# A hybrid attention block with a SwiGLU layer on one core: row sums fetched ahead through another queue, and eight score products at full width

## The chip, the cores and the metric

The kernel runs on one core of a Trainium2 chip. The metric is the device time of one execution in microseconds. The engines are named as in the profile: PE is TensorE, with PEld for its weight loads, DVE is VectorE, ACT is ScalarE, POOL is GpSimd and SP is SyncE, which here only issues DMAs.

## The reference

One decoder layer on 256 tokens of width 2048, float32. The input is normalised and projected once. One part of the projection feeds four heads of gated linear attention, another eight heads of sparse attention. Both outputs go through one output projection, and a SwiGLU layer with 5632 hidden columns follows. Cut to what matters here:

```python
n = rms_norm(x, attn_norm_g)
proj = n @ w_in
...
# gated linear attention, per chunk: b is the running sum of the log decay
decay = exp(where(causal, b[t] - b[s], -inf))
scores = einsum('bhtd,bhsd,bhtsd->bhts', qi, ki, decay)
...
h = x + concatenate([gla_out, nsa_out], axis=-1) @ w_out
m = rms_norm(h, ffn_norm_g)
return h + (silu(m @ w_gate) * (m @ w_up)) @ w_down
```

## The kernel before

**Numbers in two parts.** Every large product is made from operands split into a high part and the rest. ScalarE writes the high part (`hi`, line 136 or 623), VectorE the rest (`lo`, line 137 or 624), and TensorE makes three products of each pair of tiles: high by high, high by low, low by high. So each weight tile passes through ScalarE, then VectorE, then TensorE.

**Order of the work.** The kernel is written as Python generators. `drive` steps a main stream of products and lets side work (`urgent`, `later`) advance between them; a third list, `background`, gives one step every so many units. A planner then lays the instructions out on the engines; where a tile pool has no free buffer, the instruction that fills the next one waits until the readers of the oldest are done.

**Linear attention.** The decay between two tokens is handled by levels. `LEVELS` is 0, 1, 2, 4, ..., 64; level 0 is the diagonal, and at level l the tokens are cut into blocks of 2 l, of which the second half looks at the first. `gla_scores` does one head and one tile of 128 tokens: two banks of four products each, one for each level, every one a 128x128 product of which a mask keeps the entries that belong to the level. At the top level, l = 64, one 64x64 corner is all that is kept, and there the product itself is cut to that corner (line 565): 64 columns of weights and 64 columns of the other operand. The corner is then copied into the scores without a mask (line 574). There are 8 such products, each two records in the trace.

**The FFN.** The hidden columns are done in eleven blocks of 512 (`fb` 0 to 10). In a block, `gate_up` goes over eight pairs of 128 rows of the weights. It uses a scheme of seven products where eight would be plain: three with the weights themselves, four with sums of weight tiles. So for each pair there are three loaded parts to split and four sums. The sums `s1` and `s2` (two tiles each) are made on VectorE (lines 1104 to 1106), except that for blocks 5 to 10 those of pairs 2, 5 and 7 (`SUMS`) have been made early, in the `background` list during the attention, and put into DRAM by `sum_rows` (line 1018, from GpSimd's queue). In those blocks the kernel fetches the finished sums (line 1099) from SP's queue, behind the loads of the same pair (`load4`, line 1041):

```python
r = load4([(w_gate[0], a, 2, fb * FB), (w_up[0], a, 1 if ready else 2, fb * FB)])
if ready:
    sums = s1, s2 = g4([2, 512]), (fw["sum"] if fw else g4)([2, 512])
    for to, part in zip(sums, ready):
        nc.sync.dma_start(to, part)
```

Buffers: `fw["sum"]` (in the trace `fsum`, for `s2`) has 2, loaded weights (`fraw`) 3, split parts (`ftwo`) 4. `g4` (in the trace `g`, for `s1`) has 24, most of which hold lasting data in the FFN. After `gate_up` of a block comes `down` of the block before: four loads of `w_down`, 96 products at line 282. The products of `gate_up` are at line 1073.

Of the kernel before, what the change touches and what calls it, by code (L numbers as in the profile page):

```python
# [15 lines left out]
P = 128  # L16
# [20 lines left out]
def kernel(  # L37
# [4 lines left out]
    nc = tc.nc  # L42
    act, mm = nc.scalar.activation, nc.tensor.matmul
# [14 lines left out]
    def slot(pool, tag, bufs, align=None):  # L58
        def f(shape, dt=F32):
            n_tiles[0] += 1  # L60
            return pool.tile([P] + list(shape), dt, tag=tag, bufs=bufs, name=f"{tag}_{n_tiles[0]}", align_bytes=align)
        return f
# [3 lines left out]
    g4, g2, g1, small = slot(gp, "g4", 24, LINE), slot(s2p, "g2", 13), slot(s1p, "g1", 7), slot(s1p, "sm", 12)  # L66

    def bank():
        n_tiles[0] += 1
        return pp.tile([P, 512], F32, tag="bank", name=f"bank_{n_tiles[0]}")  # L70
# [21 lines left out]
    def drain(queue):  # L92
        while queue:
            for _ in queue.pop(0):
                pass
# [20 lines left out]
    def weight(tag, nk, w, bufs, dt=F32R):  # L116
        n_tiles[0] += 1
        if tag == "raw":
            t = wp.tile([P, 4 * 536], dt, tag=tag, bufs=bufs, name=f"{tag}_{n_tiles[0]}")
            return t[:, :nk * w].rearrange("p (k w) -> p k w", w=w)  # L120
        line = LINE // 4
        t = wp.tile([P, 2, 9 * line], dt, tag=tag, bufs=bufs, name=f"{tag}_{n_tiles[0]}", align_bytes=LINE)
        return t[:, :nk, :w]
# [432 lines left out]
    def gla_scores(h, b, res):  # L556
        tb = slice(b * P, (b + 1) * P)
        sc, e = g1([P]), dec[h // 2]
        for half in range(2):
            p = bank()  # L560
            for j in range(4):
                l = LEVELS[4 * half + j]
                u, w = (e[l][:, h % 2, tb],) * 2 if l else (kT[:, h, tb], qT[:, h, tb])
                if 2 * l == P:
                    mm(p[:l, j * P + l:(j + 1) * P], u[:, :l], w[:, l:], start=True, stop=True)
                else:
                    mm(p[:, j * P:(j + 1) * P], u, w, start=True, stop=True)  # L567
                yield
            for j in range(4):
                l, pl = LEVELS[4 * half + j], p[:, j * P:(j + 1) * P]  # L570
                if l == 0:
                    TT(sc, pl, lmask[:, 0, :], ALU.mult)
                elif 2 * l == P:
                    nc.vector.tensor_copy(sc[:l, l:], pl[:l, l:])
                else:
                    nc.vector.copy_predicated(sc, lmask[:, 4 * half + j, :].bitcast(mybir.dt.uint32), pl)
        res["s"] = sc
# [423 lines left out]
    row_sums = {}  # L1001
# [22 lines left out]
    fw = {}  # L1024

    def ffn_pools():
        nonlocal g2, small
        for pool in (wp, s2p, s1p, cp):
            pool.release()
        fr = ctx.enter_context(tc.tile_pool(name="fr", bufs=1, reuse_waits="tile"))  # L1030
        fs = ctx.enter_context(tc.tile_pool(name="fs", bufs=1, reuse_waits="tile"))
        fp = ctx.enter_context(tc.tile_pool(name="fp", bufs=1, reuse_waits="tile"))
        fw["sum"] = slot(fs, "fsum", 2)
        fw["raw"], fw["two"] = slot(fr, "fraw", 3, LINE), slot(fp, "ftwo", 4, LINE)
        g2, small = slot(fs, "f2", 6), slot(fs, "fm", 4)

    def load4(parts):

        r, at = fw["raw"]([4, 512]) if fw else weight("raw", 4, 512, 3, F32), 0
        for mat, k0, nk, c0 in parts:  # L1040
            nc.sync.dma_start(r[:, at:at + nk], mat[k0 * P:(k0 + nk) * P, c0:c0 + 512].rearrange("(k p) w -> p k w", p=P))
            at += nk
        return r
# [14 lines left out]
    def parts_of2(s1, s2):  # L1058
# [2 lines left out]
            in_parts(hi[:, 2 * i:2 * i + 2], lo[:, 2 * i:2 * i + 2], v)  # L1061
        return [(hi[:, k], lo[:, k]) for k in range(4)]


    banks = {}

    def gate_up(fb):
        def product(q, a, w, k):

            if q not in banks:  # L1070
                banks[q] = bank()
            for x, m in ((a[0], w[k][0]), (a[0], w[k][1]), (a[1], w[k][0])):
                mm(banks[q], x, m, start=todo[q] == total[q], stop=todo[q] == 1)  # L1073
                todo[q] -= 1

        def tokens(k, t):
            assert k in turned
            return tuple(x[k // 4][:, k % 4, t * P:(t + 1) * P] for x in (hT_h, hT_l))

        order, sevens = (ORDER0, ORDER1, ORDER)[0 if fb == 0 else 1 if fb < ALL7 else 2], FIRST7.get(fb, PAIRS7)  # L1080
        last7 = max(sevens, key=order.index)
        todo = dict.fromkeys((1, 5, 6, 7), 3 * len(sevens))
        todo.update(dict.fromkeys((2, 3, 4), 3 * len(sevens) + 6 * (8 - len(sevens))))
        todo[8] = 6 * (8 - len(sevens))
        total = dict(todo)
        if fb > 1:
            urgent.append(turn_act(fb - 1, (8, 8)))
        for at, pair in enumerate(order):
            if fb > 1 and pair not in sevens:
                drain(urgent)  # L1090
            if fb == 0 and at == len(OLD):
                ffn_pools()
            a, b = 2 * pair, 2 * pair + 1
            ready = row_sums.get((fb, pair))
            r = load4([(w_gate[0], a, 2, fb * FB), (w_up[0], a, 1 if ready else 2, fb * FB)])
            if ready:
                sums = s1, s2 = g4([2, 512]), (fw["sum"] if fw else g4)([2, 512])
                for to, part in zip(sums, ready):
                    nc.sync.dma_start(to, part)
            if pair in sevens:  # L1100
                w = parts_of(r[:, 0:3])
                if not ready:
                    s1, s2 = g4([2, 512]), fw["sum"]([2, 512])
                    TT(s1, r[:, 1:3], r[:, 3:4].to_broadcast([P, 2, 512]), ALU.add)  # L1104
                    TT(s2[:, 0], s1[:, 1], r[:, 1], ALU.add)  # L1105
                    TT(s2[:, 1], s2[:, 0], r[:, 0], ALU.add)  # L1106
                f = [tuple(forms[pair][:, i, j] for i in range(2)) for j in range(4)]
                raw = {1: (tokens(b, 0), 1), 2: (tokens(a, 0), 0), 3: (f[3], 2)}
                of_sums = {5: (f[0], 0), 7: (f[2], 1), 6: (f[1], 2), 4: (tokens(a, 1), 3)}

                for q in (6, 1, 5, 7, 2, 3, 4) if at == 7 else (1, 2, 3, 5, 7, 6, 4):
                    if q in of_sums and len(of_sums) == 4:
                        ws = parts_of2(s1, s2)
                        if ready:
                            ws = [ws[k] for k in (1, 0, 3, 2)]
                    if q in raw:
                        x, k = raw[q]
                        product(q, x, w, k)
                    else:
                        x, k = of_sums.pop(q)  # L1120
                        product(q, x, ws, k)
                    yield 2
            else:
                w = parts_of(r)
                for q, t, m in ((2, 0, 0), (3, 0, 1), (4, 1, 0), (8, 1, 1)):
                    for j in range(2):
                        product(q, tokens(a + j, t), w, 2 * m + j)
                        yield 2
            if pair == last7:
                q1, u, q5u, q7u, q57u = (g2([512]) for _ in range(5))  # L1130
                act(q1, banks[1], AF.Copy)
                TT(u, banks[6], q1, ALU.add)
                TT(q5u, banks[5], u, ALU.subtract)
                TT(q7u, banks[7], u, ALU.add)  # L1134
                TT(q57u, banks[5], q7u, ALU.subtract)
                if fb == 1:
                    urgent.append(turn_act(0, (1, 5)))
                if fb:
                    seed(0, DOWN[min(fb - 1, 1)])
        if fb == 0:  # L1140
            drain(urgent)
            rms(rf, ssh)
            TT(rf, rf, hback, ALU.mult)
        gs = hidden[fb] = []
        for t, (g, gq, u_, uq) in enumerate(((q1, 2, q5u, 3), (q7u, 4, q57u, 8))):
            TT(g, banks[gq], g, ALU.add)
            act(g, g, AF.Silu, scale=rf[:, t:t + 1])
            if total[uq]:
                TT(u_, banks[uq], u_, ALU.add)
            STT(g, u_, rf[:, t:t + 1], g, ALU.mult, ALU.mult)  # L1150
            gs.append(g)
# [184 lines left out]
```

## Time and profile before

| | before |
|---|---|
| median of 3 runs | 1117.23 us (1116.94 to 1117.36) |
| profiled execution | 1116.86 us, span 1115.2 us |
| TensorE busy | 1106.1 us, 99% of the span |
| VectorE busy | 993.3 us, 89% |
| ScalarE busy | 741.0 us, 66% |
| GpSimd busy | 50.1 us, 4% |
| granted TensorE clock | 1.00 |
| moved by DMA | 265.39 MB, mean 238 GB/s |

In rows of the timeline the first column is the start in us from the span's start, the second the length, then engine, line, operation, tiles and count; what stands in brackets is how long the engine sat idle before it and who ended that. In rows that group a line's instructions, three durations are the least, the median and the greatest in ns. `PEld` rows are weight loads, which overlap the products. `SPq` is SP's queue.

### The profile page before, as it was taken

How to read it: one execution, taken by the hardware profiler on the slowest of the kernel's cores; microseconds unless marked ns; L12 is line 12 of the kernel's file. 1: busy time of each engine (PE TensorE's matmuls, PEld its weight loads, DVE VectorE, ACT ScalarE, POOL GpSimd, SP SyncE). 2: the span in 40 equal slices, each digit the busy share in tenths (PEclk: the TensorE clock that was granted, in tenths of full speed). 3: DMA queues.
4: the chain of work that ended last, by engine and by line, in shares of the span. 5: the costliest groups of instructions: out<-in, count | busy, mean ns of one | idle time of the engine just before them, and what ended most of it. 6: DMA issues, size and time to landing. Idle time of an engine off the chain costs nothing.

```text
span 1115.2 us, 14712 instructions
## 1 busy us (share of the span) xinstructions
PE 1106.1 (99%) x5354; PEld 908.0 (81%) x5354; DVE 993.3 (89%) x1294; ACT 741.0 (66%) x1001; POOL 50.1 (4%) x97
## 2 busy tenths in 40 slices
PE   9999999999999999999999999999999999999998
PEld 8888887898778887887888888888888788888886
DVE  6678779987588889999899999899999999999997
ACT  7655557544576486657586676768686776768694
POOL 3110000111001000000000000000000000000000
PEclk9999999999999999999999999999999999999999
DMA  7999984475884786646465746767666767766763
GB/s 272 346 343 368 354 284 167 136 247 179 274 303 165 240 303 223 239 175 236 154 214 178 244 159 212 249 227 249 233 245 237 262 207 274 256 245 229 250 226 113
DMA packets 127795, 265.39 MB, mean 238 GB/s; under 512 B 6838, under 2 KB 8922, under 8 KB 127723
## 3 DMA queue, kind: packets, MB, share of 16 engines
q1 hardware_dynamic: 121642, 244.50, 63.4%
q0 software_dynamic: 5184, 18.88, 4.2%
q10 hardware_dynamic: 896, 1.07, 0.3%
q8 instruction: 42, 0.69, 0.2%
q14 instruction: 31, 0.25, 0.1%
HBM read 243.45 MB, written 20.97 MB: 237 GB/s over the span
## 4 chain that ended last, share of the span: by engine, by line
PE 94%; DVE 2%; ACT 2%; DMA 1%; issue 1%; POOL 0%; ACTq 0%; POOLq 0%; DVEq 0%
PE bank L282 46%; PE bank L1073 39%; PE bank L209 3%; PE bank L1214 2%; PE bank L883 1%; PE bank L567 1%; DVE lo L137 1%; PE bank L821 1%; DMA raw<-in_w_in_dram 1%; DMA raw<-in_w_out_dram 0%; ACT hi L136 0%; PE bank L737 0%; ACT ftwo L623 0%; POOL sm L212 0%; PE bank L824 0%
## 5 line engine op out<-in xcount | busy, mean ns | idle before, releaser
L1073 PE MATMUL bank<-ftwo,g 128*128 128x512 f32 x1848 | 431.7, 393 | 0.2 <-ACT ftwo L623 0.2
L1073 PEld LDWEIGHTS bank<-ftwo,g 128*128 128x128 f32 x1848 | 342.0, 188 | 77.1 <-DVE ftwo L624 3.1
L282 PE MATMUL bank<-hi,g 128*128 128x512 f32 (+2 forms) x1088 | 323.5, 376 | 0.0
L624 DVE TENSOR_TENSOR ftwo<-fraw,ftwo 128x1536 fp32r<-128x1536 f32 (+1 forms) x130 | 256.9, 1983 | 7.1 <-ACT ftwo L623 6.1
L623 ACT ACTIVATE ftwo<-fraw 128x1536 fp32r<-128x1536 f32 (+1 forms) x130 | 216.4, 1669 | 26.5 <-DMA fraw<-in_w_up_dram 10.0
L282 PE MATMUL bank<-ftwo,g 128*128 128x512 f32 x960 | 221.2, 390 | 0.4 <-ACT g L623 0.4
L282 PEld LDWEIGHTS bank<-hi,g 128*128 128x128 f32 x1088 | 192.4, 188 | 30.7 <-issue 1.0
L282 PEld LDWEIGHTS bank<-ftwo,g 128*128 128x128 f32 x960 | 179.5, 188 | 39.4 <-ACT bank L1185 1.3
L136 ACT ACTIVATE hi<-raw 128x1024 fp32r<-128x1024 f32 (+3 forms) x124 | 130.1, 1056 | 106.4 <-PE bank L282 62.7
L282 PE MATMUL bank<-lo,g 128*128 128x512 f32 (+3 forms) x544 | 195.3, 377 | 1.2 <-DVE lo L137 1.0
L137 DVE TENSOR_TENSOR lo<-raw,hi 128x1024 fp32r<-128x1024 f32 (+3 forms) x124 | 150.1, 1218 | 37.1 <-ACT hi L136 32.3
L623 ACT ACTIVATE ftwo<-g 128x1024 fp32r<-128x1024 f32 x74 | 78.3, 1058 | 75.9 <-DVE g L1104 60.4
L282 PEld LDWEIGHTS bank<-lo,g 128*128 128x128 f32 x544 | 98.5, 188 | 16.9 <-DVE lo L137 2.0
L624 DVE TENSOR_TENSOR ftwo<-g,ftwo 128x1024 fp32r<-128x1024 f32 x74 | 90.3, 1220 | 15.7 <-ACT ftwo L623 15.7
L624 DVE TENSOR_TENSOR ftwo<-fsum,ftwo 128x1024 fp32r<-128x1024 f32 x74 | 90.3, 1220 | 0.3
L623 ACT ACTIVATE ftwo<-fsum 128x1024 fp32r<-128x1024 f32 x74 | 77.6, 1050 | 4.5 <-DVE fsum L1106 3.3
L1197 ACT COPY g<-bank 128x512 f32<-128x512 f32 x80 | 46.0, 587 | 43.8 <-PE bank L282 41.9
L1104 DVE TENSOR_TENSOR g<-fraw 128x1024 f32<-128x1024 f32 x54 | 65.3, 1219 | 0.3 <-issue 0.3
L1185 ACT COPY bank<-g 128x512 f32<-128x512 f32 x80 | 45.0, 590 | 10.7 <-DVE f L1134 9.1
L623 ACT ACTIVATE g<-bank 128x512 fp32r<-128x512 f32 (+1 forms) x50 | 29.0, 591 | 32.8 <-PE bank L209 22.3
L1106 DVE TENSOR_TENSOR fsum<-fsum,fraw 128x512 f32<-128x512 f32 x54 | 37.2, 688 | 0.8
L1105 DVE TENSOR_TENSOR fsum<-g,fraw 128x512 f32<-128x512 f32 x54 | 37.1, 688 | 0.8
(235 smaller groups left out, 873.8 us busy)
## 6 DMA issues: line engine op xcount, KB each, us to landing
fraw<-in_w_gate_dram SPq DMA_DIRECT2D x86, 512.0 KB, 3.7
fraw<-in_w_down_dram SPq DMA_DIRECT2D x42, 1024.0 KB, 5.1
raw<-in_w_in_dram SPq DMA_DIRECT2D x36, 1024.0 KB, 6.9
fraw<-in_w_up_dram SPq DMA_DIRECT2D x68, 512.0 KB, 4.7
sums<-g POOLq DMA_DIRECT2D x36, 512.0 KB, 6.6
raw<-in_w_out_dram SPq DMA_DIRECT2D x16, 1024.0 KB, 6.2
g<-in_w_gate_dram SPq DMA_DIRECT2D x18, 512.0 KB, 7.6
g<-in_w_up_dram SPq DMA_DIRECT2D x18, 512.0 KB, 8.2
```

The costliest lines, as they stand in the source:

```text
L136: act(h[:, i:i + n], r[:, k + i:k + i + n], AF.Copy)
L137: last["d"] = TT(o[:, i:i + n], r[:, k + i:k + i + n], f32(h[:, i:i + n]), ALU.subtract)
L209: return nc.tensor.transpose(o, i, ident[:n, :n])
L282: last["mm"] = mm(bk[t], a[:, k, t * P:(t + 1) * P], m[:, off:off + w], start=(first_ and k == 0 and i == 0), stop=(end and k == 3 and i = ...
L623: act(hi, ps, AF.Copy)
L624: last["d"] = TT(lo, ps, f32(hi), ALU.subtract)
L1073: mm(banks[q], x, m, start=todo[q] == total[q], stop=todo[q] == 1)
L1104: TT(s1, r[:, 1:3], r[:, 3:4].to_broadcast([P, 2, 512]), ALU.add)
L1105: TT(s2[:, 0], s1[:, 1], r[:, 1], ALU.add)
L1106: TT(s2[:, 1], s2[:, 0], r[:, 0], ALU.add)
L1185: nc.scalar.copy(banks[qs[n][t]], h_sb[n][:, t, :])
L1197: nc.scalar.copy(h_sb[n][:, t, :], bs[t])
```

## The change

The top-level scores are made like the other levels, as full 128x128 products; the copy of the 64x64 corner stays. The fetch of the finished sums moves out of the pair's own step into a helper, `fetch_sums`, which is called one pair earlier, ahead of that pair's loads, takes the two tiles then, and issues both DMAs from GpSimd's queue. The pair that uses them finds its tiles in `fetched`. For a pair whose sums are not stored the helper does nothing.

```diff
@@ gla_scores
                 u, w = (e[l][:, h % 2, tb],) * 2 if l else (kT[:, h, tb], qT[:, h, tb])
-                if 2 * l == P:
-                    mm(p[:l, j * P + l:(j + 1) * P], u[:, :l], w[:, l:], start=True, stop=True)
-                else:
-                    mm(p[:, j * P:(j + 1) * P], u, w, start=True, stop=True)
+                mm(p[:, j * P:(j + 1) * P], u, w, start=True, stop=True)
                 yield
@@ ahead of gate_up
+    fetched = {}
+
+    def fetch_sums(fb, pair):
+
+        if (fb, pair) in row_sums:
+            to = fetched[fb, pair] = g4([2, 512]), fw["sum"]([2, 512])
+            for a, part in zip(to, row_sums[fb, pair]):
+                nc.gpsimd.dma_start(a, part)
@@ gate_up
             ready = row_sums.get((fb, pair))
+            if at < 7:
+                fetch_sums(fb, order[at + 1])
             r = load4([(w_gate[0], a, 2, fb * FB), (w_up[0], a, 1 if ready else 2, fb * FB)])
             if ready:
-                sums = s1, s2 = g4([2, 512]), (fw["sum"] if fw else g4)([2, 512])
-                for to, part in zip(sums, ready):
-                    nc.sync.dma_start(to, part)
+                s1, s2 = fetched.pop((fb, pair))
             if pair in sevens:
```

## The prediction

> **What bounds the kernel now.** I read the page first, then the chain of work that ended last, then busy time by stretch, then short stretches of the timeline. From the page, the span, the busy line and the chain's shares by engine:
>
> ```profile
> span 1115.2 us, 14712 instructions
> ...
> PE 1106.1 (99%) x5354; PEld 908.0 (81%) x5354; DVE 993.3 (89%) x1294; ACT 741.0 (66%) x1001; POOL 50.1 (4%) x97
> ...
> PE 94%; DVE 2%; ACT 2%; DMA 1%; issue 1%; POOL 0%; ACTq 0%; POOLq 0%; DVEq 0%
> ```
>
> TensorE carries 94% of the chain. A busy TensorE need not be at its peak, so the next view is the chain in order of time (start, length, what, count), in three of the blocks of the FFN that use stored sums:
>
> ```profile
> 822.16 22.11 PE bank L282 x96
> ...
> 883.68 22.11 PE bank L282 x96
> ...
> 966.99 3.54 PE bank L1073 x15
> ...
> 974.19 32.20 PE bank L1073 x141
> 1006.39 21.79 PE bank L282 x96
> 1028.18 3.54 PE bank L1073 x15
> ```
>
> 96 products of the down projection take 21.79 us, 227.0 ns each; 141 of gate and up take 32.20 us, 228.4 ns each. One block is 1028.18 - 966.99 = 61.19 us. At 227.0 ns the 141 would take 32.01 us and the 15 would take 3.41, so 0.19 + 0.13 = 0.32 us of a block is left to win; two blocks have a down stretch of 22.11 instead of 21.79, 0.32 more each. With six such blocks that is 6 x 0.32 + 2 x 0.32 = 2.6 us, all that faster feeding could ever bring there. Busy time by stretch (PE, PEld, DVE, ACT, POOL, clock, DMA share, GB/s) shows who is next:
>
> ```profile
> 920.00:980.00 60.00, 60.00 (x269) 48.94 (x268) 58.64 (x54) 44.35 (x50) 0.00 (x0) 1.00 0.71 250
> ```
>
> VectorE is busy 58.64 of 60 us, nearly as full as TensorE. So in these blocks the two are level: time taken from VectorE or from the transfers wins almost nothing, and time lost on VectorE costs soon. POOL is empty.
>
> **The scores.** Eight products (4 heads by 2 token tiles) of 64x64 become 128x128. Each is two records in the trace. By width alone this is a loss; the durations of one record, first from the line with the narrow product, then from the line with the full ones:
>
> ```profile
> L565 PE MATMUL bank<-g x16: 222/246/270, 181.9 to 257.5; 128*64 128x64 f32 x16
> ```
> ```profile
> L567 PE MATMUL bank<-g x96: 270/274/377, 172.5 to 256.9; 128*128 128x128 f32 x96
> ```
>
> 274 - 246 = 28 ns over 16 records is +0.45 us. But durations overlap; what counts is from one start to the next. The timeline of TensorE around one of each:
>
> ```profile
> 180.93 0.39 PE L282 MATMUL bank<-hi,g 128*128 128x512 f32 x1
> 181.16 0.38 PE L567 MATMUL bank<-g 128*128 128x128 f32 x2
> 181.30 0.48 PE L282 MATMUL bank<-lo,g 128*128 128x512 f32 x1
> 181.62 0.38 PE L567 MATMUL bank<-g 128*128 128x128 f32 x2
> ...
> 183.44 0.40 PE L282 MATMUL bank<-hi,g 128*128 128x512 f32 x1
> 183.77 0.33 PE L565 MATMUL bank<-g 128*64 128x64 f32 x2
> 184.03 0.50 PE L282 MATMUL bank<-hi,g 128*128 128x512 f32 x1
> 184.36 0.38 PE L567 MATMUL bank<-g,g 128*128 128x128 f32 x2
> ```
>
> Around the full product: 0.23 before it, 0.14 for it, 0.32 after the next, 0.69 us from 180.93 to 181.62. Around the narrow one: 0.33, 0.26 and 0.33, 0.92 us from 183.44 to 184.36. The narrow one is dearer by 0.23 us, 0.10 on going in and 0.12 on coming out. The rows of the weight loads show why:
>
> ```profile
> 181.27 0.19 PEld L282 LDWEIGHTS bank<-lo,g 128*128 128x128 f32 x1
> 181.38 0.43 PEld L567 LDWEIGHTS bank<-g 128*128 128x128 f32 x2
> ...
> 183.77 0.19 PEld L565 LDWEIGHTS bank<-g 128*64 128x64 f32 x2 [0.36 <-issue]
> 184.03 0.19 PEld L282 LDWEIGHTS bank<-hi,g 128*128 128x128 f32 x1
> ```
>
> Full forms load ahead of their products (181.38 for 181.62, 181.27 for 181.30); the narrow one loads only as it starts (183.77), after 0.36 us for which the profile shows no wait, and so does the one behind it (184.03). Eight of them make 8 x 0.23 = 1.84 us saved. The ends are +0.45 (the durations) and -1.84; I take -1.84, since starts are what the next product sees and the neighbours are the same line.
>
> The Trainium skill, page TensorEngine Tiling (Array Packing), section Key Properties, says that changing the tiling mode drains TensorE. By that rule each narrow product costs two drains and the full form none, the sign of the -1.84; the same page's table of speedups for dimensions of 64 would, taken alone, promise a loss from widening, and the starts above speak against it.
>
> These products lie in the linear attention's stretch, woven into the input projection, where the chain runs on TensorE. VectorE copies the same 64x64 corner afterwards, so it pays nothing. What follows (the later projections, the output projection, the FFN) starts from TensorE's progress, so I let the whole 1.84 reach the end. Were VectorE's queue there to end last instead, nothing would: the bound is 0. The new lengths also shift a few neighbours in the built order of this stretch (evictions and norms by a place or two); the work is the same, and I put it at 0 +- 0.4, about two products.
>
> **The sums.** 36 fetches of 512 KB (6 blocks, 3 pairs, 2 halves) leave SP's queue for POOL's and are asked for one pair ahead. How long each held SP, how long it took to land from SP, and how long the writes of the same tiles, which already go through POOL's queue, took there:
>
> ```profile
> L1099 SPq DMA_DIRECT2D fsum<-sums x18: 326/339/343, 718.3 to 1053.9; - x18
> ...
> DMA to landing us min/median/max: 4.0/5.6/7.5
> ```
> ```profile
> L1018 POOL DMA_DIRECT2D sums<-g x36: 531/531/720, 42.7 to 432.2; - x36
> ...
> DMA to landing us min/median/max: 2.9/6.6/9.6
> ```
>
> SP is relieved of 36 x 0.34 = 12 us of issuing and of the waits for a free buffer, and the weight loads behind them can go earlier. That is worth what anyone waits for such loads in these blocks. From the waits between 740 and 1100 us (total, times, longest):
>
> ```profile
> PEld bank L1073 <- DVE ftwo L624: 2.1, 11, 0.3
> ...
> ACT ftwo L623 <- DMA fraw<-in_w_down_dram: 0.3, 1, 0.3
> ```
>
> One wait of 0.3 us. POOL gains 36 x 0.53 = 19 us of issuing, in a stretch where it has nothing; queued behind a waiting fetch there is only the next fetch.
>
> What else moves: both halves of the sums have two buffers to turn in. Pair 2 now takes its buffers ahead of pair 1, so pair 1 waits for pair 0's, pair 3 for pair 2's, 4 for 3's, 6 for 4's, where they alternated. The built order of VectorE changes by single places for it. The timeline of a block, at pair 2, where it changes most:
>
> ```profile
> 903.27 0.34 SPq L1099 DMA_DIRECT2D fsum<-sums  x1
> ...
> 907.46 1.23 DVE L624 TENSOR_TENSOR ftwo<-g,ftwo 128x1024 fp32r<-128x1024 f32 x1 [0.97 <-ACT ftwo L623]
> 907.48 0.47 SPq L1099 DMA_DIRECT2D g<-sums  x1
> ...
> 913.20 1.22 DVE L624 TENSOR_TENSOR ftwo<-fsum,ftwo 128x1024 fp32r<-128x1024 f32 x1
> ...
> 916.26 1.22 DVE L624 TENSOR_TENSOR ftwo<-g,ftwo 128x1024 fp32r<-128x1024 f32 x1
> ...
> 923.00 1.22 DVE L1104 TENSOR_TENSOR g<-fraw 128x1024 f32<-128x1024 f32 x1
> ```
>
> Now the first half comes late (asked for at 907.48), so its split stands at 916.26, behind pair 3's additions; after, it stands near 913.2 and the additions behind it. From 907.46, where VectorE last idles (0.97 us, set by TensorE's pace), to 923.00 it has the same instructions, and ScalarE's halves come in time in both orders, so 923.00 stays. What is moved ahead of 907.46 has that 0.97 us of idle time as its cover. In the last block one addition (1.22 us) moves ahead of two splits; TensorE may lose some tenths there once. I put the sums at 0, between -2.6 (all of the reserve above) and the lateness that the next part prices.
>
> **Sum.** Against the profiled execution (1116.86 us, 1.7 over its span): 1116.86 - 1.84 + 0 = 1115.0. The median of the runs before, 1117.23, lies 0.37 higher, so the forecast is 1117.23 - 1.84 = 1115.4 us. I count as no change what lies within 0.2%, 2.2 us, about what a measurement of this kernel can tell: 1115.0 to 1119.5.
>
> **Rivals.** *Pair 7's sums come late* (the slow side). They cannot be asked for before pair 5's splits give the buffers back, now as after:
>
> ```profile
> 930.87 0.33 SPq L1099 DMA_DIRECT2D g<-sums  x1
> ...
> 932.01 0.33 SPq L1099 DMA_DIRECT2D fsum<-sums  x1
> ...
> 938.19 1.04 ACT L623 ACTIVATE ftwo<-g 128x1024 fp32r<-128x1024 f32 x1
> ...
> 940.18 1.22 DVE L624 TENSOR_TENSOR ftwo<-g,ftwo 128x1024 fp32r<-128x1024 f32 x1
> ```
>
> Asked at 930.87, used by ScalarE at 938.19; VectorE's turn at 940.18 leaves 0.95 us over after ScalarE's 1.04. It decides from 7.3 + 0.95 = 8.3 us of landing. POOL's queue took 6.6 at the median but 9.6 at worst, when the transfers were denser than here. At 9.6 every block loses 1.3 us, straight on TensorE, since VectorE has no gap left before the block's end: 6 x 1.3 = 7.8, so 1115.4 + 7.8 = 1123.2. Against it: the median leaves 1.7 us. In the Trainium skill, page SBUF — State Buffer, section "SBUF: two separate sides", stands a rule against this change: while VectorE runs an operation in its two-port mode, GpSimd cannot write the descriptors of its DMAs, and they start late. It would act as this rival; the operations in these blocks are additions and subtractions of two tensors, beside which the 36 writes landed as shown, and no run here shows a two-port one in their way.
>
> *TensorE's remaining waits in the blocks go too.* The reserve of 2.6 us, half of it 1.3: 1114.1, at best 1112.8. For it: the splits of pair 2 come 3 us earlier, and loads move up. Against: the waits are on VectorE's splits at a block's end (11 times, 2.1 us), whose amount of work stays.
>
> *The scores bring nothing*, because VectorE ends last in that stretch, or the durations and not the starts tell: 1117.2 to 1117.7.
>
> *The fetches don't go ahead in fact*, because POOL's queue waits for the same buffers. True for pair 7 by the rows above; for pairs 2 and 5 nobody waits now, so it changes no number.
>
> **How the numbers follow.** The forecast (scores -1.84, sums about 0) 0.48, its own range 1114.6 to 1116.4; a third of it lies under 1115.0. Waits going too 0.25. Scores worth nothing 0.12. Late sums 0.15, anything from 1119 on. Faster: 0.25 + 0.15 = 0.40; the same: 0.33 + 0.12 = 0.45; slower: 0.15. The range of 8 in 10 runs from 1113.2 (the waits with a little over half the reserve) to 1119.0 (where the late sums begin to tell).
>
> **What would show it.** Right: no record of 128x64 is left in the attention, and from one projection product to the next around a top-level score 0.69 instead of 0.92 us; the chain's blocks still 61.2 us; the sums' fetches on POOL landing under 8 us; SP's waits without those of the fetches. Wrong: blocks over 61.5 us with ScalarE waiting for a DMA of sums at pair 7 (late sums), blocks under 60.9 (waits gone), or the FFN's first product starting as late as now though the scores are cheaper.

## The result, and the profile after

The changed kernel takes 1115.86 us (median of 22 runs, 1114.58 to 1117.10) beside 1117.45 us of the kernel before (22 runs): ratio 0.9986, 95% interval 0.9980 to 0.9992, 1.6 us less. Two repeats gave 1.50 and 1.54 us less (0.9983 and 0.9987). By the bound of the prediction, 0.2%, that is "the same", on the fast side. The forecast was 1115.4 us.

The profiled execution of the changed kernel took 1115.98 us. From its page, the span, the busy line and the chain's shares by engine:

```profile
span 1114.3 us, 14723 instructions
...
PE 1103.7 (99%) x5354; PEld 907.3 (81%) x5354; DVE 992.6 (89%) x1294; ACT 742.1 (67%) x1001; POOL 69.4 (6%) x133
...
PE 86%; DMA 5%; DVE 4%; ACT 2%; issue 1%; SPq 0%; ACTq 0%; DVEq 0%
```

TensorE still carries the chain. POOL has grown by 19.3 us, the 36 issues of 0.53 us. Three blocks of the FFN in the chain, in order of time (start, length, what, count):

```profile
904.94 3.52 PE bank L1079 x15
...
912.12 32.31 PE bank L1079 x141
944.43 21.81 PE bank L282 x96
966.24 3.52 PE bank L1079 x15
...
973.42 32.31 PE bank L1079 x141
1005.73 21.81 PE bank L282 x96
1027.54 3.52 PE bank L1079 x15
```

A block is 966.24 - 904.94 = 61.30 us, where before had 61.19: the 141 products take 32.31 instead of 32.20. What TensorE's weight loads wait for in such a block, and the waits between 740 and 1100 us (total, times, longest):

```profile
928.79 10.30 PEld L1079 LDWEIGHTS bank<-ftwo,g 128*128 128x128 f32 x46 [0.27 <-DVE ftwo L621]
939.34 1.69 PEld L1079 LDWEIGHTS bank<-ftwo,g 128*128 128x128 f32 x8 [0.25 <-DVE ftwo L621]
```
```profile
PEld bank L1079 <- DVE ftwo L621: 3.0, 12, 0.3
...
ACT ftwo L620 <- DMA fraw<-in_w_down_dram: 0.6, 1, 0.6
```

The waits for VectorE's splits grew from 2.1 to 3.0 us. So the FFN got a little slower, and the gain is elsewhere. TensorE's timeline around the place that the prediction showed with a narrow score (hi, score, hi, score):

```profile
184.04 0.39 PE L282 MATMUL bank<-hi,g 128*128 128x512 f32 x1
184.26 0.38 PE L564 MATMUL bank<-g 128*128 128x128 f32 x2
184.40 0.48 PE L282 MATMUL bank<-hi,g 128*128 128x512 f32 x1
184.72 0.38 PE L564 MATMUL bank<-g,g 128*128 128x128 f32 x2
```

184.72 - 184.04 = 0.68 us, where before had 0.92. No record of 128x64 is left on the line of the scores.

To place the gain I use one more number, the **stretch**: the time from the first wide (512 columns) projection product after 170 us of the kernel before to the 179th after it, worked out from the start times in each trace. It spans the linear attention's scores. It is 92.17 us before and 89.95 after: 2.22 us less. It hardly varies: a second trace of the kernel before gave 92.23, two more of the changed one 89.89 and 89.90.

### The profile page after: what moved, and what is told of

Same layout as the page of the kernel before. It is cut to its first block, busy times and chain, and to the rows that moved or that the text cites. A ratio compares the mean times of both kernels' runs of the same rounds, so it can differ in the third digit from the quotient of the medians.

```text
span 1114.3 us, 14723 instructions
## 1 busy us (share of the span) xinstructions
PE 1103.7 (99%) x5354; PEld 907.3 (81%) x5354; DVE 992.6 (89%) x1294; ACT 742.1 (67%) x1001; POOL 69.4 (6%) x133
## 4 chain that ended last, share of the span: by engine, by line
PE 86%; DMA 5%; DVE 4%; ACT 2%; issue 1%; SPq 0%; ACTq 0%; DVEq 0%
PE bank L282 41%; PE bank L1079 35%; PE bank L209 3%; DMA g<-in_w_up_dram 2%; PE bank L1220 2%; DVE ftwo L621 1%; DMA raw<-in_w_in_dram 1%; PE bank L564 1%; DMA raw<-in_w_out_dram 1%; DVE lo L137 1%; PE bank L880 1%; ACT ftwo L620 1%; PE bank L818 1%; ACT hi L136 1%; DMA fraw<-in_w_down_dram 1%
## 5 line engine op out<-in xcount | busy, mean ns | idle before, releaser
L282 PE MATMUL bank<-hi,g 128*128 128x512 f32 (+1 forms) x1088 | 323.4, 376 | 1.2 <-ACT hi L322 1.2
L1068 POOL DMA_DIRECT2D g<-sums x18 | 9.6, 533 | 554.9 <-DVE ftwo L621 526.3
```

Of the source, the lines that this page charges most:

```text
L282: last["mm"] = mm(bk[t], a[:, k, t * P:(t + 1) * P], m[:, off:off + w], start=(first_ and k == 0 and i == 0), stop=(end and k == 3 and i = ...
```

## The experiments

All times below are medians beside runs of the kernel before on the same chip. The ratio is not in every row exactly that of the two medians (scores only again: 0.9990, and 0.9993 from the medians). "Block" is from the row of 15 products near 905 us to the next near 966 in the chain, as above, and from there to the next where the chain has that row; a semicolon parts one trace from the next.

| kernel | less (-) or more than before, us | ratio, 95% interval | stretch, us | block, us |
|---|---|---|---|---|
| before; again | | | 92.17; 92.23 | 61.20, 61.19; 61.19, 61.21 |
| changed; again; third | -1.59; -1.50; -1.54 | 0.9986; 0.9983; 0.9987 | 89.95; 89.89; 89.90 | 61.30, 61.30; 61.26, 61.32; 61.28, 61.34 |
| scores only; again | -1.71; -0.74 | 0.9977 to 0.9994; 0.9981 to 0.9998 | 89.94; 89.98 | 61.16; 61.21 |
| sums only | +0.49 | 0.9994 to 1.0013 | 92.20 | 61.29, 61.28 |
| full weights, 64 moving | -0.46 | 0.9985 to 1.0003 | 90.41 | 61.24 |
| 64 weights, full moving | +1.70 | 1.0004 to 1.0022 | 92.58 | 61.20, 61.21 |
| ahead, from SP | +0.78 | 0.9996 to 1.0013 | 89.93 | 61.34, 62.98 |
| not ahead, from GpSimd | -0.84 | 0.9982 to 1.0000 | 89.91 | 61.26 |
| ahead in the last block; again | -2.11; -1.99 | 0.9972 to 0.9989; 0.9970 to 0.9987 | 89.93; 89.93 | 61.19, 61.20; 61.21, 61.22 |

### The two halves of the change

Scores only, from the kernel before:

```diff
-                if 2 * l == P:
-                    mm(p[:l, j * P + l:(j + 1) * P], u[:, :l], w[:, l:], start=True, stop=True)
-                else:
-                    mm(p[:, j * P:(j + 1) * P], u, w, start=True, stop=True)
+                mm(p[:, j * P:(j + 1) * P], u, w, start=True, stop=True)
```

> The kernel before with the eight top-level scores as full 128x128 products and nothing else. Theory A (the gain of the whole change is the scores', the sums cost a little in the FFN's blocks): 1.8 to 2.3 us less than the kernel before, so more than the whole change brought (1.56 us); the blocks of the FFN stay at 61.19 us; around a top-level score 0.69 us instead of 0.92. Theory B (the scores brought part and the sums the rest): 0.8 us less or nothing. Theory C (the scores' place in the order shifted its neighbours, and the form itself is indifferent): a gain, but 0.9 us still around the product.

Sums only: the changed kernel with these lines as they were before.

> The kernel before with the sums' fetches one pair ahead from GpSimd's queue and nothing else; the scores stay narrow. Theory A: 0.2 to 0.7 us more than the kernel before, six blocks of 61.30 us instead of 61.19, with TensorE waiting 0.25 us for VectorE's splits at 24 and 34.6 us of a block. Theory B: 0.8 to 1.5 us less. If the 0.11 us of a block in the changed kernel was chance: no difference, blocks of 61.19.

Scores only: 1.71 us less, stretch 89.94, block 61.16. Sums only: 0.49 us more (its interval includes no change), stretch 92.20, block 61.28 to 61.29. Each part does in its own place what the whole change does there: theory A. The gain of the scores alone lies just under the 1.8 to 2.3 us expected, and a repeat below brought less still; part of it is lost in the last block, as shown there. The chain with the sums only (line 1082 is the line of the gate and up products there):

```profile
906.67 3.52 PE bank L1082 x15
...
967.96 3.52 PE bank L1082 x15
```

### What makes the narrow score dear

Two kernels give the narrow product one full side each. Half of each result is not used.

```diff
-                    mm(p[:l, j * P + l:(j + 1) * P], u[:, :l], w[:, l:], start=True, stop=True)
+                    mm(p[:, j * P + l:(j + 1) * P], u, w[:, l:], start=True, stop=True)
```

> The kernel before, only that the narrow top-level score takes all 128 columns as weights and keeps 64 columns of the moving operand (the other half of the result is not used). If the 64 weight columns are what costs (the array changes its form, and weights cannot be loaded ahead): 0.65 to 0.69 us around it, 1.8 to 2.4 us less than before in all, as good as the full product or a little better. If any product of another width than its neighbours' pays: 0.9 us around it and no gain.

```diff
-                    mm(p[:l, j * P + l:(j + 1) * P], u[:, :l], w[:, l:], start=True, stop=True)
+                    mm(p[:l, j * P:(j + 1) * P], u[:, :l], w, start=True, stop=True)
```

> The kernel before, only that the narrow top-level score keeps 64 columns of weights and takes all 128 columns of the moving operand (half of the result is not used). If the 64 weight columns cost: 0.92 to 0.98 us around it as in the kernel before, its weights loaded only as it starts, and the time of the kernel before, up to 0.4 us more. If the moving width costs: 0.69 us around it and 1.8 us less.

TensorE with full weights and 64 moving columns, then with 64 weight columns and the full moving operand, the same place in both; the last row is the weight load of the second:

```profile
184.21 0.39 PE L282 MATMUL bank<-hi,g 128*128 128x512 f32 x1
184.44 0.33 PE L565 MATMUL bank<-g 128*128 128x64 f32 x2
184.58 0.48 PE L282 MATMUL bank<-hi,g 128*128 128x512 f32 x1
184.89 0.38 PE L567 MATMUL bank<-g,g 128*128 128x128 f32 x2
```
```profile
184.13 0.40 PE L282 MATMUL bank<-hi,g 128*128 128x512 f32 x1
184.46 0.43 PE L565 MATMUL bank<-g 128*64 128x128 f32 x2
184.82 0.50 PE L282 MATMUL bank<-hi,g 128*128 128x512 f32 x1
185.16 0.38 PE L567 MATMUL bank<-g,g 128*128 128x128 f32 x2
```
```profile
184.46 0.19 PEld L565 LDWEIGHTS bank<-g 128*64 128x64 f32 x2 [0.37 <-issue]
```

With full weights 0.68 us, as for the full product; with 64 weight columns 1.03 us, more than the 0.92 of the 64x64 product, and its load starts only with the product, 0.37 us after the one before. So the columns of the weights cost: with all 128 of them, the width that moves does not matter here. And 64 moving columns save nothing: the next wide product starts 0.14 us after the score (184.58 - 184.44), exactly as behind the full one (184.40 - 184.26). In the Trainium skill, page TensorEngine Tiling (Array Packing), section Key Properties, stands that a change of the tiling mode drains TensorE; these rows agree, with 0.24 us for the 64x64 product and 0.35 for the 64x128 one, though what they show is weights loaded late and not a drain itself.

The stretches then separate form from order. The records of TensorE up to 262 us stand in the same order in the kernel before and with full weights; and in one other order, the same for both, with full products and with 64 weight columns. In the first order the form is worth 92.17 - 90.41 = 1.76 us, 0.22 for each of eight. In the second it is worth 92.58 - 89.94 = 2.64, 0.33 each, against the 64x128 form. Between the two orders, with forms that cost the same, lie 90.41 - 89.94 = 0.47 us. One wait shows most of it. It is in the kernel before and with full weights, and in none of the kernels with the second order whose rows I read there (scores only, 64 weights, changed again):

```profile
218.51 0.51 PE L282 MATMUL bank<-lo,g 128*128 128x256 f32 x2 [0.30 <-DVE lo L137]
```
```profile
218.38 0.51 PE L282 MATMUL bank<-lo,g 128*128 128x256 f32 x2 [0.29 <-DVE lo L137]
```

The medians of these two kernels are worse guides than their traces: with full weights only 0.46 us was gained, where the stretch gives 1.76. At the end of its last block it lost 1.1 us at one product to a late load, a place where kernels below lose time too. With 64 weight columns the time is 1.70 us more, where up to 0.4 was expected and the stretch gives 0.41. The traced execution, 1117.43 us, was the fastest of its eleven, so what the others lost beyond that stays open.

### The lead or the queue

The change to the fetches has two parts: the lead, one pair ahead, and the queue, GpSimd's. Fetched one pair ahead, but from SP's queue:

```diff
-                nc.gpsimd.dma_start(a, part)
+                nc.sync.dma_start(a, part)
```

> The changed kernel with the sums still asked for one pair ahead, but from SP's queue again; the order of instructions on TensorE, VectorE and ScalarE is that of the changed kernel to the last one. Theory lead (asking ahead turns the order of buffers and so of VectorE's splits, and that costs 0.1 us a block, whichever queue asks): blocks of 61.28 to 61.30 us, the intervals of 0.33 us on TensorE at 24.0 and 34.6 us of a block are still there. Theory queue (GpSimd's queue and its landing times cost it): blocks of 61.17 to 61.19 us and those intervals gone. The median between 0.5 us less and 0.8 us more than the changed kernel's; more, if the loads of w_down at the end come late again behind SP's fetches, by 0.4 to 1.2 us at one place near 1066 us.

Full scores, fetched in the pair's own step, but from GpSimd's queue:

```diff
                 for to, part in zip(sums, ready):
-                    nc.sync.dma_start(to, part)
+                    nc.gpsimd.dma_start(to, part)
```

> Full scores, and the sums fetched in the pair's own step as in the kernel before, but from GpSimd's queue. Theory lead: blocks of 61.17 to 61.19 us, as with SP, and 0.3 to 0.7 us less than the changed kernel, 1.9 to 2.5 us less than the kernel before: the best of all. Theory queue: blocks of 61.28 to 61.30 us and the changed kernel's time. At the end of the last block TensorE does not wait for w_down (in the kernel with full scores alone it waited 0.4 us there, with the narrow-moving scores 1.2 us), because SP's queue holds no fetch in front of those loads.

Ahead from SP: block 61.34 (the next, 62.98, holds a stop of 1.3 us told below), so the lead and not the queue lengthens the block. In time it is far worse than the changed kernel, 0.78 us over the kernel before, more than I had allowed, and not near 1066 us. Its first large loss in these blocks, in SP's queue, then ScalarE's longest wait for data between 740 and 1100 us; and SP's queue at the same place in the changed kernel:

```profile
802.68 0.34 SPq L1068 DMA_DIRECT2D g<-sums  x1
803.06 0.43 SPq L1038 DMA_DIRECT2D fraw<-in_w_up_dram  x1
805.57 0.33 SPq L1068 DMA_DIRECT2D fsum<-sums  x1
805.95 15.03 SPq L1038 DMA_DIRECT2D fraw<-in_w_down_dram  x4
```
```profile
819.66 1.92 ACT L620 ACTIVATE ftwo<-fraw 128x2048 fp32r<-128x2048 f32 x1 [1.36 <-DMA fraw<-in_w_down_dram]
```
```profile
802.13 0.47 SPq L1038 DMA_DIRECT2D fraw<-in_w_up_dram  x1
804.58 16.54 SPq L1038 DMA_DIRECT2D fraw<-in_w_down_dram  x4
```

A fetch that waits for its buffer (802.68, 805.57) holds what stands behind it: the load of `w_up` goes out at 803.06 instead of 802.13, the first of `w_down` at 805.95 instead of 804.58. ScalarE then waits 1.36 us for a load of `w_down`, and TensorE stops for 1.0 us at 822 us. Two blocks later, just before 1007.79, it stops for 1.3 us more. The two kernels differ in the queue alone, so the queue costs the time; that it does so through these held loads is read from the rows. From GpSimd's queue the same early fetches hold nothing.

Not ahead, from GpSimd: 61.26 us for the block, between the two groups, so this number alone doesn't decide; all blocks with the lead lie at 61.26 to 61.34 (mean of nine 61.30, without the one with the stop), all without it at 61.16 to 61.26 (mean of fourteen 61.21). The start times do decide: at one product 24 us into the block (below), every kernel with the lead has an interval of 0.335 to 0.341 us in each of the first five blocks, and every kernel without it, this one too, 0.28 at most. The expectation of 1.9 to 2.5 us less failed, it was 0.84 less. It did not avoid a wait in the last block either. ScalarE's wait there, and the chain's piece that ended it:

```profile
1050.04 1.06 ACT L620 ACTIVATE ftwo<-fsum 128x1024 fp32r<-128x1024 f32 x1 [1.46 <-DMA fsum<-sums]
```
```profile
1045.02 5.00 DMA fsum<-sums
```

The sums in the last block come late here though GpSimd's queue asks; with SP asking they do too (below). What counts is that they are asked for in the pair's own step.

How the lead lengthens the block: VectorE's splits come no later. The split behind the wait at 928.79 in the changed kernel, and the same one with the scores alone, whose block starts at 904.10:

```profile
927.52 1.22 DVE L621 TENSOR_TENSOR ftwo<-fsum,ftwo 128x1024 fp32r<-128x1024 f32 x1
```
```profile
904.10 3.54 PE bank L1070 x15
```
```profile
926.78 1.22 DVE L621 TENSOR_TENSOR ftwo<-fsum,ftwo 128x1024 fp32r<-128x1024 f32 x1
```

It starts 22.58 us after the block's start with the lead (927.52 - 904.94) and 22.68 without. But the lead changes TensorE's own list too. At both places of the block where a product's weights wait for a split, one product that waits for nothing and stood in front of it stands behind it now, so TensorE comes to the waiting product one place sooner (0.227 us). The weight loads with the scores alone, to set beside those of the changed kernel at 928.79 and 939.34:

```profile
928.05 10.30 PEld L1070 LDWEIGHTS bank<-ftwo,g 128*128 128x128 f32 x46 [0.16 <-DVE ftwo L621]
938.61 4.43 PEld L1070 LDWEIGHTS bank<-ftwo,g 128*128 128x128 f32 x20 [0.25 <-DVE ftwo L621]
```

At the first place the load is held up 0.27 us instead of 0.16, and by the start times the next product follows after 0.337 us instead of 0.233. At the second place both wait 0.25 us, and both have 0.33. So the first place alone costs 0.10 us, which is what the block is longer. This holds in the first five of the six blocks. In the last the list is another and the 141 products take no longer, first the changed kernel, then the kernel before:

```profile
1034.72 32.21 PE bank L1079 x141
```
```profile
1035.38 32.20 PE bank L1073 x141
```

This cause is read from the lists and the traces; no kernel was run that changes this order alone.

### The last block alone

> Full scores; the sums are fetched one pair ahead from GpSimd's queue in the last block of the FFN alone, and in the pair's own step from SP's queue in the five blocks before it. If the lead costs 0.1 us in each block and pays only in the last one (where without it ScalarE waits 0.5 to 1.5 us for the sums at 1050 us): five blocks of 61.17 to 61.20 us, no wait for the sums near 1050, and 0.4 to 0.6 us less than the changed kernel, 2.0 to 2.2 us less than the kernel before. If the blocks' 0.1 us was made up for elsewhere by GpSimd's queue: the changed kernel's time or more.

```diff
-            if at < 7:
+            if at < 7 and fb == 10:
                 fetch_sums(fb, order[at + 1])
...
             if ready:
-                s1, s2 = fetched.pop((fb, pair))
+                if fb == 10:
+                    s1, s2 = fetched.pop((fb, pair))
+                else:
+                    sums = s1, s2 = g4([2, 512]), (fw["sum"] if fw else g4)([2, 512])
+                    for to, part in zip(sums, ready):
+                        nc.sync.dma_start(to, part)
```

Beside it ran the kernel before, the scores alone and the changed kernel, once more each, without an edit.

> The kernel before once more, for a second look: how far two executions of the same program differ, and where. If the shifts of 0.2 to 1.0 us that the runs show before 100 us are chance of the first transfers: this one starts its products at 160 us 0 to 1.0 us later than the first look. If they belong to the change: within 0.1 us of the first look. The wait of ScalarE for the sums at the last block's middle (0.5 us in the kernel with full moving operand, none in the first look) may be there or not.

> The kernel with full scores alone once more, beside the changed kernel on the same chip. If the lead's gain at the end of the last block and its cost of 0.1 us in each block cancel: both within 0.4 us. If the wait for the sums near 1050 us and the one for w_down near 1066 us belong to the program and not to the execution: both are here again, 0.7 to 1.5 us and 0.4 to 1.2 us.

> The changed kernel once more: blocks of 61.28 to 61.30 us, no wait for the sums and none for w_down in the last block, the stretch of the linear attention 2.2 us shorter than in the kernel before, and 1.2 to 2.0 us less than that kernel in all.

Ahead in the last block alone: 2.11 us less than the kernel before, 0.61 less than the changed kernel; its blocks in the chain (between 740 and 1100 us it has no wait for a DMA on ScalarE):

```profile
905.17 3.54 PE bank L1079 x15
...
966.36 3.54 PE bank L1079 x15
```

The scores alone gave 0.74 us less this time (1114.0 to 1118.8), 0.76 more than the changed kernel on the same chip, where both were expected within 0.4. The two waits are here again. ScalarE with the scores alone, first trace (two rows) and second (two rows):

```profile
1049.51 1.06 ACT L620 ACTIVATE ftwo<-fsum 128x1024 fp32r<-128x1024 f32 x1 [0.88 <-DMA fsum<-sums]
...
1063.43 1.92 ACT L620 ACTIVATE ftwo<-fraw 128x2048 fp32r<-128x2048 f32 x1 [0.80 <-DMA fraw<-in_w_down_dram]
```
```profile
1049.97 1.06 ACT L620 ACTIVATE ftwo<-fsum 128x1024 fp32r<-128x1024 f32 x1 [0.93 <-DMA fsum<-sums]
...
1066.72 1.92 ACT L620 ACTIVATE ftwo<-fraw 128x2048 fp32r<-128x2048 f32 x1 [0.33 <-DMA fraw<-in_w_down_dram]
```

In the chain of the second trace the piece "DMA fsum<-sums" of 4.80 us at 1045.15 is followed by VectorE, then by a load of `w_down` of 6.89 us asked for at 1059.74, then by TensorE: the late sums hold VectorE, VectorE gives a buffer of loaded weights back late, and so the next load is late. TensorE loses 0.64 us there in the first trace and 0.97 in the second against the kernel before, from start to start. In all, ScalarE waited for sums in the middle of the last block in five of the seven traces that fetch there in the pair's own step (0.5 to 1.5 us), and in none of the seven that fetch ahead there. The two traces without it are those of the kernel before; why it escapes stays open.

The kernel before once more differs from its own first trace too. The waits of VectorE between 60 and 110 us (total, times, longest), first trace and second:

```profile
DVE g L1014 <- DMA g<-in_w_up_dram: 4.9, 1, 4.9
```
```profile
DVE g L1014 <- DMA g<-in_w_up_dram: 5.4, 1, 5.4
```

Its products stood 0.5 us later at 160 us and 1.5 later at 310 us; 0.85 of that comes in one step at 295 us, and between 262 and 312 us ScalarE's waits for loads of `w_out` grew from 10.7 to 11.4 us. In the last block it has no wait for the sums, only one of 0.5 us in the first of the six blocks. So what the traces show before 170 and from 290 to 310 us differs from one execution to the next, in part at least by the landing of loads, and is not to be put down to the change.

The last two, on one chip:

> The kernel that fetches ahead in the last block alone, once more, beside the changed kernel on the same chip. If the 0.1 us of each block is all that tells the two apart: 0.3 to 0.7 us less than the changed kernel again, 1.9 to 2.3 us less than the kernel before, and no wait for the sums or for w_down near the end. If the first look was luck: within 0.2 us of the changed kernel.

> The changed kernel beside it: 1.4 to 1.7 us less than the kernel before, as in the two looks so far (1.56 and 1.50), with blocks of 61.28 to 61.30 us.

1115.05 and 1115.50 us beside 1117.04: 1.99 and 1.54 less, as expected. Near the end ScalarE had a wait of 0.3 us for `w_down` that was not expected. It cost TensorE 0.1 us at most: from the last block's first product to the last of all it took 82.72 us, and 82.62 in the first trace of this kernel. Both repeats of each kernel together, 22 runs each: 1115.13 against 1115.76 for the changed kernel, 0.6 us; drawing the 22 runs of each side anew many times, 95% of the differences lie between -1.1 and 0.0. It is the best version seen, by a margin that these runs only just show.

## Why the prediction was right, and where not

**The scores** were right in kind and place. 0.23 us each was predicted from starts and not from durations; full weights alone gave 0.22. The end at +0.45 (durations) is out, and so is "the scores bring nothing". The term that was too small is the order: put at 0 +- 0.4, it came to -0.47, mostly since a wait of TensorE for VectorE (0.30) went. The stretch gained 2.2 instead of 1.84.

**The sums** were put at 0, with a gain of up to 2.6 or lateness as ends. They cost 0.095 us in each of five blocks and nothing in the sixth, 0.48 us. On TensorE, from the first product of the first of these blocks to the last product of all, the four traces with the lead and GpSimd's queue in every block take 389.4 to 389.7 us (mean 389.53), the three without the lead whose last block loses nothing (the kernel before twice, 64 weight columns) 388.9 to 389.3 (mean 389.09): some 0.4 us. The step that failed is "the built order of VectorE changes by single places", from which I argued that the end of VectorE's work stays. It does stay; I did not look at what the same change does to TensorE's own list, which puts a waiting product one place further ahead. Sum: -2.2 + 0.5 = -1.7, where 1.50 to 1.59 less was measured. So the forecast of 1115.4 was near 1115.86 in part because two misses of opposite sign nearly cancel.

**Landing** was as forecast for POOL's queue (under 8 us), as the line of the fetches has it (with the sums only, one fetch took 8.5 us, and nobody waited for it):

```profile
DMA to landing us min/median/max: 3.5/4.6/7.7
```

**Late sums of pair 7**, the slow rival, rested on a wrong claim: that they cannot be asked for before pair 5's splits. They take pair 4's buffers. In the changed kernel, at the block that the prediction showed:

```profile
926.14 0.53 POOL L1068 DMA_DIRECT2D g<-sums  x1 [9.79 <-DVE ftwo L621]
929.03 0.53 POOL L1068 DMA_DIRECT2D fsum<-sums  x1 [2.37 <-DVE ftwo L621]
```

The kernel before asked at 930.87 and 932.01: 4.7 and 3.0 us later, 0.85 of it because its block starts later (905.79 against 904.94). ScalarE uses the second half at 938.17 in the changed kernel, so even a landing of 8.5 us is in time. The rival deserved far less than 0.15. Lateness existed, but on the other side: without the lead, in the last block, when the sums are fetched in the pair's own step. The trace of before could not show it: neither trace of that kernel has the wait.

**The waits going too**: the opposite happened, 3.0 us instead of 2.1. **The last block** was to lose some tenths; with the change it lost none, and it is the block where the lead pays, beside full scores without it.

**The fetches not going ahead**, true for pair 7 as I put it, was wrong there as well, and for the same reason.

**Two small readings** were off too. Of the range 1114.6 to 1116.4 only 0.4 of 1.8 us lies under 1115.0, less than the third that the chances go by. And 1113.2 stands for 2.2 of the reserve of 2.6 us, which is most of it and not a little over half.

## What to carry to other kernels

A lone product with fewer weight columns than its neighbours can cost more than the full one: read it from start to start, with the weight loads beside it, before cutting work out of a product. When a fetch is moved ahead, read the order of every engine anew, not only of the one that uses it: a product moved by one place cost more here than the fetch saved, except in the last block, where data came late without the lead. Fetch ahead only where a trace shows someone waiting, and from a queue in which nothing urgent stands behind the fetch.

## What was not expected of the hardware

A product with 64 weight columns costs more when more columns move (1.03 against 0.92 us around it), while with full weights 64 and 128 moving columns cost the same (0.68). A weight load that is held up costs the product behind it little and then no more than 0.11 us. In the blocks of the FFN, where the usual interval from start to start is 0.227 to 0.236 us, the next product followed after 0.233 us when the load was held 0.16, after 0.249 at 0.17, 0.274 at 0.20, 0.331 at 0.25 and 0.337 at 0.27; behind stops of TensorE with loads held 0.42 and 1.39 us it was 0.335 both times. And one execution of the same program differs from the next by up to 1.5 us in the first 310 us, as much as the whole change.
